# The pace of a projection stream in a chunked-scan block: one period for all steps, or one by the width of the step

## The chip, the cores and the metric

The kernel runs on one core of a Trainium2 chip. The metric is the device time of one execution in microseconds (us). Engines are named as in the profile: PE is TensorE (PEld its weight loads), DVE is VectorE, ACT is ScalarE, POOL is GpSimd, SP is SyncE, which issues the DMAs.

## What is computed

One layer of a diffusion block over 2048 latent tokens with a prefix of 256 context tokens, width 1024. One input projection feeds three groups of heads, whose outputs are joined, projected and followed by an MLP:

```python
zl = modulate(rms_norm(xl, p["norm1_g"]), ml[0], ml[1]) @ p["w_in"]
zl_gla, zl_rwkv, zl_ret = split_cols(zl, (GLA_COLS, RWKV_COLS, RET_COLS))
yl_gla, _ = gla_mixer(zl_gla, p, st_gla, True)          # gated linear attention, 4 heads
yl_rwkv, _ = rwkv7_mixer(zl_rwkv, p, st_rwkv, True, rows)  # RWKV-7, 6 heads
yl_ret, _ = retnet_mixer(zl_ret, p, st_ret, True, True)    # retention, 4 heads
xl = xl + ml[2] * (jnp.concatenate([yl_gla, yl_rwkv, yl_ret], axis=-1) @ p["w_out"])
hl = modulate(rms_norm(xl, p["norm2_g"]), ml[3], ml[4])
xl = xl + ml[5] * squared_relu_mlp(hl, p["mlp_w1"], p["mlp_w2"])
return rms_norm(xl, final_norm_g)
```

Each mixer scans the tokens forward and backward; the latent scans start from the final context states.

## The kernel before

The program has three parts: the modulation with that share of the input projection which RWKV needs first (to about 578 us of the span), the scans (to about 2075 us), and the output projection with the MLP (the rest). The change lies in the scans.

In the scans several generators write their instructions into one program, a step at a time: `prepare` (per direction, RWKV blocks: tiles `pg`, `p`, `M`, `X`, `XT`, `GB`, `BKT`), `chains` (the sequential RWKV chunks: `ptf`, `ptb`, `Ts`, `SUV`, `UV`, `py`), `inputs` (RWKV features of the second and third pair of heads: `px`, `pv`, `po`, `pl`), `finish` (`pm`, `pn`, `pgt`), `mix` (the GLA heads, `gpA`, `gpy`, `gpt`, `gz`, then two pairs of retention heads, `rpk`, `rpt`, `rpA`, `rpy`, with `fpt` at a head's end), and `ip_stream`, the projection stream of the title. All their matmuls have line L1068, that of a helper, so that the tiles' names tell them apart.

`ip_stream` (L445) computes the columns of the projection that GLA and retention need late: values, gates, and the retention's keys, values and queries. It goes through five groups of columns, `STREAM_T` (L442), and in each through the 18 tiles of 128 tokens (16 where context tokens aren't needed). Groups 0, 1, 2 and 4 are 384 columns wide (in 2 and 4 the two context tiles have 256), group 3 is 256 wide. For a tile it loads `rh` (512 KB, the saved normalized tokens as two fp16 parts; two buffers), makes 24 fp16 matmuls into `pz` (one buffer) with the weights `rwh` and `rwl`, scales `pz` to `rzs` on ACT and stores that to `zt` in DRAM. A `yield` after every sixth matmul makes four steps of a tile. The low half of a group's weights, `rwl`, is loaded into the buffer that the group before has just left (L454, three buffers).

An object of class `Order` (L1042) picks whose step is written next. It keeps a time `t` of its own, which grows with each matmul by a cost that goes by its columns. The other streams are picked by their position and by when their last step should be done. The projection stream has a `period`: it is taken when it is due, and ahead of that only where nothing else is ready and it is due within three periods:

```python
for s in paced:
    if s.due <= self.t or len(open_) == 1:
        return s
...
for s in paced:
    if s.due <= self.t + 3 * s.period:
        return s
...
if s.period:
    s.due = max(s.due, self.t - s.period) + s.period
```

`mix` waits for groups: the GLA heads for group 0, their last step (`follow`) for group 1, the first retention pair for the tiles of group 2 and at its end for group 3, the second pair for the tiles of group 4. What the generators write is then recorded by the framework, which may still move an instruction within an engine's order.

Of the kernel before, what the change touches and what calls it, by code (L numbers as in the profile page):

```python
# [366 lines left out]
def ip_tile(k, nm, wp, ps, tag="pn"):  # L367

    srcs, M, _ = CT[nm]
    wh = wp.tile([P, KD, P], F16, tag="wh", name="wh", bufs=3)  # L370
    wl = wp.tile([P, KD, P], F16, tag="wl", name="wl", bufs=3)
    return wh, wl, ip_weights(k, wp, ps.tile([P, 512], F32, tag=tag, name="pnrm")[:, 0:1], wh[:, :, 0:M], wl[:, :, 0:M], srcs, M)
# [59 lines left out]
def h_save(k, first):  # L432

    for ti in range(NT):
        with k.tc.issue_after(k.stores[first + ti]):
            for i, h in enumerate((k.hh, k.hl)):
                k.nc.sync.dma_start(k.hd[ti, :, i], h[:, :, ti * P : ti * P + P])
# [9 lines left out]
def ip_stream(k, wp, ps):  # L447


    nc = k.nc  # L450

    def weights(g, i):
        w = wp.tile([P, KD, 384], F16, tag="rw", name="rw" + "hl"[i], bufs=3)
        nc.sync.dma_start(w[:, :, 0 : P * len(STREAM_T[g])], k.wsd[g][i])  # L454
        return w

    wh = weights(0, 0)
    for g, cols in enumerate(STREAM_T):
        W, kind = P * len(cols), cols[0][2]
        wl = weights(g, 1)  # L460
        if g == 0:
            yield 8
        for ti in range(2 if kind == "g" else 0, NT):
            n = 256 if ti < 2 and kind == "r" else W
            if ti == NT - 1:
                nxt = weights(g + 1, 0) if g + 1 < len(STREAM_T) else None
            h = wp.tile([P, 2, KD, P], F16, tag="rh", name="rh", bufs=2)
            nc.sync.dma_start(h, k.hd[ti])
            pz = ps.tile([P, 512], F32, tag="fl", name="pz")
            i = 0  # L470
            for a, b in ((0, wh), (0, wl), (1, wh)):
                for kk in range(KD):
                    nc.tensor.matmul(pz[:, 0:n], h[:, a, kk, :], b[:, kk, 0:n], start=(i == 0), stop=(i == 23))
                    i += 1
                    if i in (6, 12, 18):
                        yield 0
            s = 1 if ti < 2 else 0
            zs = wp.tile([P, 384], F32, tag="rzs", name="rzs", bufs=2)
            for u in range(n // P):
                nc.scalar.activation(zs[:, P * u : P * u + P], pz[:, P * u : P * u + P], AF.Copy, scale=k.siv[:, g, u, s : s + 1])  # L480
            z = zs[:, 0:n]
            if kind == "g":
                th = wp.tile([P, 384], F32, tag="rth", name="rth")[:, 0:n]
                nc.scalar.activation(th, z, AF.Tanh, scale=0.5)
                nc.gpsimd.tensor_scalar(th, th, 0.5, 0.5, ALU.mult, ALU.add)
                nc.gpsimd.tensor_mul(z, z, th)
            nc.sync.dma_start(k.zt[ti * P : (ti + 1) * P, cols[0][1] : cols[0][1] + n], z)
            k.tile = ti + 1
            yield 0
        k.streamed, k.tile = k.streamed + 1, 0  # L490
        wh = nxt
# [57 lines left out]
def rw_weights(k, cp):  # L549

    nc = k.nc
    k.w3 = cp.tile([96, 3, 384], F32R, name="w3")
    with k.tc.tile_pool(name="rws", bufs=1) as tp:
        t = tp.tile([96, 3, 384], F32, name="w3f")
        for i, w in enumerate((k.I["rwkv_w2"][0, 0], k.I["rwkv_w2"][0, 1], k.I["rwkv_a2"][0])):
            for p in range(3):
                nc.sync.dma_start(t[32 * p : 32 * p + 32, i, :], w)
        stacked_rhs(nc, k.w3, t)
# [472 lines left out]
class Stream:  # L1031
# [5 lines left out]

    def pos(self):
        return self.first + (self.last - self.first) * self.done / self.count


class Order:  # L1042
# [1107 lines left out]
def tile_hybrid_block(ctx: ExitStack, tc: tile.TileContext, I, cst_ap, off, out):  # L2150
    nc = tc.nc
    k = K()
# [22 lines left out]
    with ExitStack() as rs:  # L2175
        rp = rs.enter_context(tc.tile_pool(name="rconst", bufs=1))
        cs = rp.tile([P, n_rw], F32, name="cst")
        nc.sync.dma_start(cs, cst_ap[:, 0:n_rw])
        k.cst = lambda n: cs[:, off[n][0] : off[n][0] + off[n][1]]
        k.gmax = rp.tile([R2, 4, NT, 2], F32, name="gmax")  # L2180
        feat = ExitStack()
        with ExitStack() as es:
            wp = es.enter_context(tc.tile_pool(name="ipw", bufs=2, side="right"))
            k.stores, k.turned, names = [], [], ["L", "G", "k0", "v0", "r0"]
            with tc.tile_pool(name="ipx", bufs=2) as xp, tc.tile_pool(name="mops", bufs=4, space=PSUM) as mps:
                ready = []
                first, rest = modulation1(k, xp, mps, lambda: ready.append(ip_tile(k, names[0], wp, mps, "pb")))
                hp, lp = (es.enter_context(tc.tile_pool(name="hT" + i, bufs=1, side="right")) for i in "hl")
                ips = es.enter_context(tc.tile_pool(name="ipps", bufs=2, space=PSUM, side="right"))
                k.hh = hp.tile([P, KD, T], F16, name="hT_hi")  # L2190
                k.hl = lp.tile([P, KD, T], F16, name="hT_lo")
                for i, bi in enumerate(TOK_ORDER):
                    h_block(k, bi, xp, None if i else first)
                    if i == 0:
                        with tc.issue_after(k.h_last):
                            rest()
                            ready.append(ip_tile(k, names[1], wp, mps, "pb"))
                    if i == 1:
                        ready.append(ip_tile(k, names[2], wp, mps, "pb"))
            k.ipn = es.enter_context(tc.tile_pool(name="ipn", bufs=1, space=PSUM, side="right"))  # L2200
            ip_channels(k, names, wp, ips, ready)
            setup(k)
            rw_setup(k, rp)
            h_save(k, 5)
            p0 = feat.enter_context(tc.tile_pool(name="rf0", bufs=1))
            p1 = feat.enter_context(tc.tile_pool(name="rf1", bufs=1))
            rw_weights(k, p0)
            rw_seg(k, p0)
            k.fb = 2
            with tc.tile_pool(name="rfb", bufs=2) as pool, tc.tile_pool(name="rfps", bufs=3, space=PSUM) as fps, tc.tile_pool(name="rbaps", bufs=1, space=PSUM) as bps:  # L2210
                rw_shared(k, pool)
                for _ in rw_inputs(k, 0, pool, pool, fps):
                    pass
                for _ in rw_base(k, 0, k.LTc, p1, bps):
                    pass
                ip_channels(k, ["k1", "v1", "r1"], wp, ips)
                modulation2(k, cp, 20)
                for _ in rw_inputs(k, 1, p1, pool, fps, 0, B1):
                    pass
                ip_channels(k, ["k2", "v2", "r2"] + GLA_COLS, wp, ips)  # L2220

        lps = rs.enter_context(tc.tile_pool(name="lps", bufs=2, space=PSUM))

        def inputs():
            pool = feat.enter_context(tc.tile_pool(name="rf", bufs=2))
            k.fb = 1
            yield from rw_inputs(k, 1, p1, pool, lps, B1)
            yield from rw_base(k, 1, k.LTc, p1, lps)
            k.inputs = 1
            yield from rw_inputs(k, 2, p1, pool, lps)  # L2230
            yield from rw_base(k, 2, k.LTc, p1, lps)
            feat.close()
            k.inputs = 2

        def mix():
            yield lambda: k.inputs == 2
            yield from mixers(k, lps)

        with ExitStack() as es:
            bp = es.enter_context(tc.tile_pool(name="rb", bufs=2, side="right"))  # L2240
            ps = es.enter_context(tc.tile_pool(name="rbps", bufs=3, space=PSUM, side="right"))
            fp = es.enter_context(tc.tile_pool(name="ipr", bufs=1, side="right"))
            fps = es.enter_context(tc.tile_pool(name="iprps", bufs=1, space=PSUM, side="right"))
            k.order, k.inputs, k.streamed, k.tile, k.fin = Order(nc), 0, 0, 0, None
            rw_scan(k, bp, ps)
            k.order.add(inputs(), 0, 108, 200, 12)
            k.mix = k.order.add(mix(), 108, 316, 270, 12)
            k.order.add(ip_stream(k, fp, fps), 0, 312, 345, period=3.1)
            k.order.run()
        gla_flag(k, cp)  # L2250
    gflag = nc.values_load(k.gflag, min_val=0, max_val=1)
# [30 lines left out]
```

## Time and profile before

| | |
|---|---|
| time, median of 3 runs | 3627.11 us (3613.73 to 3627.25) |
| the profiled execution: its time / span | 3641.55 us / 3639.4 us |
| mean granted clock of TensorE | 0.913 |
| busy: PE, DVE, ACT, POOL | 92%, 66%, 39%, 19% |
| PE records (an fp32 matmul is two) | 23600 |

The profile is of one execution. PE is busy nearly all the time, but a busy PE is not PE at its full clock: where the granted clock is 0.50, the chip runs TensorE at 1.2 of its 2.4 GHz, and the same matmuls take about twice as long. So the scans are read by stretches, each with its length, PE's busy time and the granted clock.

### The profile page before, as it was taken

To read this page: it belongs to the slowest core of one execution; us is meant where nothing else is said; L and a number is where in the kernel's file an instruction comes from. 1 tells how busy PE (TensorE), PEld (TensorE's weight loads), DVE (VectorE), ACT (ScalarE), POOL (GpSimd) and SP (SyncE) were. 2 spreads that over 40 slices of the span, in tenths; PEclk is the share of its full clock that TensorE was granted. 3 is DMA by queue.
4 is the path that set the end of the run, shared out by engine and by line. 5 is a ranking of instruction groups with operands and counts; after the bars stand their busy time and mean duration, and the time that the engine had idled before them with its cause. 6 is when DMAs were issued, how large, how long until landed. Compare 5 with 4: busy or idle time off the path is not lost. (4 is left out here: it accounts for less than half of the span.)

```text
span 3639.4 us, 62904 instructions
## 1 busy us (share of the span) xinstructions
PE 3362.6 (92%) x23600; PEld 2257.2 (62%) x23600; DVE 2388.7 (66%) x5128; ACT 1427.0 (39%) x3161; POOL 685.8 (19%) x863
## 2 busy tenths in 40 slices
PE   6798999998998999999999689799999999999997
PEld 2444445666675667777676577556666666666665
DVE  7458784767865667666656378777777764454446
ACT  3355553444434464443434234444433441122113
POOL 3224442324522223323222100000000010000001
PEclk7898999999987988778998599899999999999998
DMA  7988877536645245242523168744433473232232
GB/s 229 201 242 247 251 213 209 162 99 194 167 140 135 78 126 147 68 110 92 151 77 102 57 195 229 241 176 142 172 141 136 155 228 116 90 118 93 90 102 89
DMA packets 534345, 547.09 MB, mean 150 GB/s; under 512 B 276603, under 2 KB 407494, under 8 KB 533262
## 3 DMA queue, kind: packets, MB, share of 16 engines
q1 hardware_dynamic: 534032, 542.99, 50.1%
q8 instruction: 188, 3.08, 0.3%
q14 instruction: 125, 1.02, 0.1%
HBM read 331.18 MB, written 187.55 MB: 143 GB/s over the span
## 5 line engine op out<-in xcount | busy, mean ns | idle before, releaser
L1938 PE MATMUL pu<-H,wo 128*128 128x512 f16 x2688 | 608.7, 380 | 1.2 <-DVE s L1946 1.2
L2125 DVE TENSOR_TENSOR acc<-acc,pz 128x512 f32<-128x512 f32 x512 | 348.6, 686 | 348.3 <-PE pz L2123 346.5
L1938 PEld LDWEIGHTS <-wo 128*128 128x128 f16 x2688 | 252.0, 98 | 320.4 <-issue 41.1
L2123 PE MATMUL pz<-w2h,uh 128*128 128x512 f32 x1024 | 425.2, 419 | 11.7 <-ACT uh L1965 10.5
L2123 PE MATMUL pz<-w2l,uh 128*128 128x512 f32 x1024 | 403.4, 394 | 0.0
L2123 PE MATMUL pz<-w2h,ul 128*128 128x512 f32 x1024 | 397.3, 391 | 0.4 <-DVE ul L1967 0.4
L1068 PE MATMUL pz<-rwh,rh 128*128 128x384 f16 (+1 forms) x1376 | 294.5, 345 | 12.6 <-DMA rh<-hd 6.2
L1068 PEld LDWEIGHTS <-rh 128*128 128x128 f16 x2064 | 200.9, 106 | 137.8 <-issue 37.0
L2139 POOL TENSOR_TENSOR acc<-acc,fg 128x1024 f32<-128x1024 f32 x10 | 23.6, 2377 | 1373.9 <-ACT acc L2138 1373.9
L2123 PEld LDWEIGHTS pz<-w2h,uh 128*128 128x128 f32 x1024 | 194.0, 189 | 65.6 <-ACT uh L1965 11.5
L2123 PEld LDWEIGHTS pz<-w2h,ul 128*128 128x128 f32 x1024 | 192.9, 188 | 42.8 <-DVE ul L1967 1.1
L2123 PEld LDWEIGHTS pz<-w2l,uh 128*128 128x128 f32 x1024 | 194.2, 190 | 40.1
L425 PEld LDWEIGHTS <-wh 128*128 128x128 f16 (+2 forms) x1072 | 111.5, 108 | 148.5 <-issue 40.8
L1962 ACT ACTIVATE u<-u 128x512 f32<-128x512 f32 x64 | 36.8, 623 | 402.9 <-DVE s L1956 402.9
L425 PE MATMUL pz<-hT_hi,wh 128*128 128x512 f16 (+5 forms) x536 | 125.1, 374 | 41.4 <-ACT zs L428 23.5
L1068 PE MATMUL pz<-rwl,rh 128*128 128x384 f16 (+1 forms) x688 | 146.1, 343 | 0.0
L1068 PE MATMUL pg<-Z,BK 64*128 64x128 f32 (+1 forms) x864 | 131.3, 329 | 3.8 <-issue 1.1
L1950 ACT ACTIVATE s<-pu,iv 128x512 f32<-128x512 f32 x96 | 65.2, 684 | 166.3 <-PE pu L1938 163.9
L2043 PE MATMUL pz<-woh,yh 128*128 128x512 f32 x256 | 100.9, 409 | 30.7 <-DMA x<-in_w_out_dram 22.0
L425 PE MATMUL pz<-hT_hi,wl 128*128 128x512 f16 (+5 forms) x536 | 123.4, 368 | 0.0
L425 PE MATMUL pz<-hT_lo,wh 128*128 128x512 f16 (+5 forms) x536 | 121.4, 365 | 0.0
L1068 PEld LDWEIGHTS pg<-Z,BK 64*128 64x128 f32 x864 | 111.4, 226 | 15.0 <-issue 6.9
(522 smaller groups left out, 6920.4 us busy)
## 6 DMA issues: line engine op xcount, KB each, us to landing
rh<-hd SPq DMA_DIRECT2D x86, 512.0 KB
st<-in_mlp_w_dram SPq DMA_DIRECT2D x64, 512.0 KB
w1d<-wo SPq DMA_DIRECT2D x112, 256.0 KB
wo<-w1d SPq DMA_DIRECT2D x112, 256.0 KB
x<-in_x_dram SPq DMA_DIRECT2D x32, 512.0 KB
mw<-in_mod_w_dram SPq DMA_DIRECT2D x32, 512.0 KB
w2d<-w2h SPq DMA_DIRECT2D x32, 512.0 KB
w2d<-w2l SPq DMA_DIRECT2D x32, 512.0 KB
```

Source lines behind the costliest of these rows:

```text
L425: nc.tensor.matmul(pz[:M, o : o + step], a[:, kk, 0:M], b[:, kk, t0 + o : t0 + o + step], start=(i == 0), stop=(i == 23))
L1068: return op(out, lhs, rhs, **kw)
L1938: nc.tensor.matmul(bank, W[o][:, a, kk], H[o][:, 4 * b + kk], start=(i == 0), stop=(i == 11))
L1950: nc.scalar.activation(s, product(o), AF.Copy, scale=iv)
L1962: nc.scalar.activation(r, r, AF.Relu)
L2043: nc.tensor.matmul(pz, a[:, kk], w[:, kk, 512 * hf : 512 * hf + 512], start=(kk + i == 0), stop=(kk == KD - 1 and i == 2))
L2123: nc.tensor.matmul(pz, U[q][tb][u][:, ts], W2[q][w][:, cs], start=(i == 0), stop=(i == 5))
L2125: nc.vector.tensor_add(a[:, cs], a[:, cs], pz)
L2139: nc.gpsimd.tensor_mul(a, a, fg)
```

## The change

The stream's period is no longer 3.1 of the planner's units for every step, but 3.3 for a step of 384 columns and 2.2 for one of 256. `ip_stream` sets it at the first step of each tile, when the due time of that step has been set already.

```diff
@@ ip_stream
         for ti in range(2 if kind == "g" else 0, NT):
             n = 256 if ti < 2 and kind == "r" else W
+            k.stream.period = PACE * n / 384
@@ before class Order
+PACE = 3.3
@@ tile_hybrid_block
-            k.order.add(ip_stream(k, fp, fps), 0, 312, 345, period=3.1)
+            k.stream = k.order.add(ip_stream(k, fp, fps), 0, 312, 345, period=PACE)
```

No instruction is added or removed; they stand in another order. Lines after L462 are one higher in the changed kernel, those after `PACE` four (the helper's L1068 is L1072). PE's matmul instructions in the scans, counted in its order from one group's last stream matmul to the next one's last:

| part of PE's order | all matmuls, before | now | of these the stream's | share of the stream, before | now |
|---|---|---|---|---|---|
| group 0 (384 wide) | 1715 | 1580 | 432 | 0.252 | 0.273 |
| group 1 (384) | 1530 | 1709 | 384 | 0.251 | 0.225 |
| group 2 (384) | 1606 | 1378 | 432 | 0.269 | 0.313 |
| group 3 (256) | 1862 | 1625 | 384 | 0.206 | 0.236 |
| group 4 (384) | 1694 | 1899 | 432 | 0.255 | 0.227 |
| behind the stream | 238 | 454 | 0 | 0 | 0 |

PE, at the change from group 0 to group 1, before; between the two stream matmuls stand 16 others:

```order
L1068 MATMUL pz<-rwh,rh 128x384
L1068 MATMUL p_8664<-XT,M_8611 64x32 x8
L1068 MATMUL py<-Z,SUVf 64x64
L1068 MATMUL ptf<-Tsf,XT 64x64 x2
L1068 MATMUL ptb<-Tsb,XT 64x64 x2
L1068 MATMUL py<-Z,SUVf 64x64
L1068 MATMUL py<-Z,SUVb 64x64 x2
L1068 LDWEIGHTS rh
```

Now, from the same stream matmul on:

```order
L1072 MATMUL pz<-rwh,rh 128x384
L1072 MATMUL pg<-Z,BK 128x128 x4
L1072 MATMUL py<-Z,SUVf 64x64
L1072 MATMUL ptf<-Tsf,XT 64x64 x2
L1072 MATMUL py<-Z,SUVf 64x64
L1072 MATMUL pv<-ident,v 128x128 x3
L1072 MATMUL ptb<-SUVb,Z 64x64 x2
L1072 MATMUL py<-Z,SUVb 64x64 x2
L1072 MATMUL ptb<-Tsb,XT 64x64 x2
L1072 MATMUL p_8449<-X,GB 64x64 x8
```

These rows are the beginning of 145 matmuls of RWKV and its features that now stand between the two groups.

PE, in group 3, the beginning of its longest run without a stream matmul, before (286 matmuls to the next one):

```order
L1068 MATMUL pz<-rwh,rh 128x256
L1068 MATMUL p_17138<-M_17066,XT 64x32 x8
L1068 MATMUL p_17149<-XT,M_17066 64x64 x8
L1068 MATMUL p_17159<-M_17101,XT 64x32 x8
L1068 MATMUL ptf<-UVf,BKT 64x64 x2
L1068 MATMUL ptb<-UVb,BKT 64x64 x2
L1068 MATMUL gpy<-gV,gAs_17350 128x96
L1068 MATMUL p_17170<-XT,M_17101 64x64 x8
```

Now the longest run of group 3 has 148:

```order
L1072 MATMUL pz<-rwh,rh 128x256
L1072 MATMUL p_16968<-X,GB 64x64 x8
L1072 MATMUL ptf<-UVf,BKT 64x64 x2
L1072 MATMUL ptb<-UVb,BKT 64x64 x2
L1072 MATMUL gpA<-gqm,gkm 128x128 x4
L1072 MATMUL py<-Z,SUVf 64x64 x2
L1072 MATMUL py<-GB,UVf 64x64 x2
L1072 MATMUL gpA<-gqm,gkm 128x128
```

The run of 286 is gone; group 3 holds the same 384 stream matmuls among 237 fewer others.

PE, behind the stream's last matmul, before:

```order
L1068 MATMUL pz<-rwh,rh 128x384
L1068 MATMUL ptf<-Tsf,XT 64x64 x2
L1068 MATMUL ptb<-Tsb,XT 64x64 x2
L1068 MATMUL fpt<-ident,rY 128x128 x4
L1068 MATMUL py<-GB,UVf 64x64
L1068 MATMUL py<-GB,UVb 64x64
L1068 MATMUL ptf<-UVf,BKT 64x64 x2
```

Now:

```order
L1072 MATMUL pz<-rwh,rh 128x384
L1072 MATMUL py<-Z,SUVf 64x64 x2
L1072 MATMUL py<-GB,UVf 64x64 x2
L1072 MATMUL rpk<-rV,rkd 64x64
L1072 MATMUL py<-Z,SUVb 64x64 x2
L1072 MATMUL py<-GB,UVb 64x64 x2
L1072 MATMUL p_21949<-M_21870,XT 64x32 x8
```

The stream now ends while RWKV blocks are still being prepared (`p`); 216 matmuls more stand behind it.

## Rows read from the trace of the kernel before

**Rows 1.** The page: the span, and busy time of each engine.

```profile
span 3639.4 us, 62904 instructions
...
PE 3362.6 (92%) x23600; PEld 2257.2 (62%) x23600; DVE 2388.7 (66%) x5128; ACT 1427.0 (39%) x3161; POOL 685.8 (19%) x863
```

**Rows 2.** The tile `rwh`: its matmuls (ns min/median/max, first and last start).

```profile
L1068 PE MATMUL pz<-rwh,rh x1376: 269/326/543, 577.7 to 1978.2; 128*128 128x384 f16 x151, 128*128 128x256 f16 x46
```

**Rows 3.** The tile `rwl`: the loads of groups 1 to 4.

```profile
L454 SPq DMA_DIRECT2D rwl<-ws1l x1: 320/320/320, 843.6 to 843.6; - x1
L454 SPq DMA_DIRECT2D rwl<-ws2l x1: 319/319/319, 1075.8 to 1075.8; - x1
L454 SPq DMA_DIRECT2D rwl<-ws3l x1: 562/562/562, 1362.6 to 1362.6; - x1
L454 SPq DMA_DIRECT2D rwl<-ws4l x1: 320/320/320, 1719.3 to 1719.3; - x1
```

**Rows 4.** Windows, one per group and the tail: length, busy us (records), clock, DMA.

```profile
core 0: us, PE busy (x) PEld busy (x) DVE busy (x) ACT busy (x) POOL busy (x), PEclk, DMA share, GB/s
577.70:843.60 265.90, 249.24 (x2752) 173.51 (x2751) 166.48 (x402) 104.87 (x335) 77.67 (x124) 0.92 0.49 139
843.60:1075.80 232.20, 217.72 (x2411) 152.21 (x2409) 182.71 (x475) 100.22 (x312) 107.24 (x137) 0.90 0.60 172
1075.80:1362.60 286.80, 261.33 (x2799) 186.78 (x2797) 185.69 (x462) 145.21 (x373) 75.08 (x111) 0.88 0.43 115
1362.60:1719.30 356.70, 331.14 (x3219) 264.62 (x3218) 242.34 (x647) 149.60 (x376) 114.11 (x159) 0.77 0.38 103
1719.30:1978.20 258.90, 250.26 (x2852) 185.86 (x2851) 150.28 (x494) 98.87 (x305) 61.08 (x68) 0.93 0.38 113
1978.20:2075.00 96.80, 77.90 (x390) 65.36 (x389) 44.89 (x139) 28.95 (x63) 19.96 (x20) 0.52 0.14 42
```

**Rows 5.** Waits of PE from 577 to 2075 us: total, times, longest.

```profile
PE fpt L1068 <- POOL rY L1477: 10.6, 4, 7.7
PE pk L1068 <- ACT sqf L781: 9.0, 3, 4.2
PE pu L1068 <- DMA gz<-gzsl: 7.2, 2, 4.2
PE pz L1068 <- DMA rh<-hd: 6.2, 4, 1.9
...
PE pz L1068 <- ACT rzs L480: 5.5, 6, 2.9
```

**Rows 6.** Windows over the longest runs without a stream matmul (columns as above).

```profile
1517.50:1577.60 60.10, 60.10 (x564) 51.25 (x564) 25.05 (x71) 11.26 (x37) 13.93 (x16) 0.57 0.22 57
1392.80:1414.10 21.30, 21.30 (x307) 18.15 (x307) 11.40 (x33) 6.31 (x18) 8.24 (x9) 1.00 0.48 93
1922.30:1941.50 19.20, 17.31 (x246) 15.12 (x247) 7.93 (x25) 4.88 (x18) 2.79 (x3) 0.80 0.30 88
```

**Rows 7.** Windows at the end of the scans (columns as above).

```profile
2000.00:2025.00 25.00, 20.25 (x89) 17.31 (x89) 16.41 (x53) 8.21 (x17) 5.82 (x7) 0.50 0.11 32
2025.00:2050.00 25.00, 25.00 (x118) 22.84 (x119) 4.14 (x8) 7.46 (x14) 2.80 (x3) 0.50 0.00 1
2050.00:2075.00 25.00, 13.23 (x60) 11.25 (x58) 9.01 (x20) 2.21 (x4) 6.89 (x5) 0.50 0.13 44
```

## The prediction, made before the changed kernel was run

> **What bounds the kernel now.** I read the page first: PE is busy for 3362.6 of 3639.4 us [rows 1], so this is a kernel whose time is PE's, and the question is where PE waits and where it runs slowly. The chain of waits ends in the last normalization and says nothing of the scans, so I cut the scans into stretches. The stream's first matmul starts at 577.7 us and its last at 1978.2 [rows 2]; the low half of each group's weights is loaded when the group before has given its buffer back, at 843.6, 1075.8, 1362.6 and 1719.3 us [rows 3]. These marks make six windows [rows 4]: five groups, and a tail in which no stream is left. PE is busy 91 to 97% of each group, and its single waits are small: the largest kind adds up to 10.6 us over the whole of the scans [rows 5]. What differs is the granted clock: 0.92, 0.90, 0.88 and 0.93 in the wide groups 0, 1, 2 and 4, but 0.77 in the narrow group 3, and 0.52 in the tail [rows 4]. At half clock (1.2 GHz) nearly every matmul takes twice as long, so the clock is what the order can gain or lose.
>
> Divided by the matmuls that stand in PE's order (the table of the change), the windows of [rows 4] cost, for each matmul: group 0 265.9/1715 = 0.155 us, group 1 232.2/1530 = 0.152, group 2 286.8/1606 = 0.179, group 3 356.7/1862 = 0.192, group 4 258.9/1694 = 0.153, the tail 96.8/238 = 0.407.
>
> **The change, part by part.** It adds no instruction. A step of 384 columns comes 3.3/3.1 = 6% later in the planner's time, one of 256 comes 29% sooner. What this does is seen in the order: group 3 sheds 237 other matmuls, the wide groups together take 21 more (6545 before, 6566 now), and the tail 216 more. Within the wide groups it is uneven: groups 1 and 4 get thinner (the stream's share falls from 0.251 and 0.255 to 0.225 and 0.227), groups 0 and 2 denser (0.252 and 0.269 to 0.273 and 0.313). So there are four terms.
>
> *(a) The wide groups.* No row shows a wide group with a share of 0.226; the nearest are groups 1 and 4 at 0.253 with a mean clock of 0.915, and group 3 at 0.206 with 0.77 [rows 4]. On the line between these, 0.027 less share costs 0.027 x 0.145/0.047 = 0.083 of clock. Groups 1 and 4 now hold 3608 matmuls at 0.152 us, 549 us; at a clock of 0.832 in place of 0.915 that is +55. The denser groups 0 and 2 hold 2958 at 552.7/3321 = 0.166 us, 492 us; at best their clock goes from 0.90 to the 0.93 of group 4, -16. Together +39 at most. At the other end stands 0: among the wide groups the rows show no slope at all (group 2 has the largest share and the lowest clock). I take **+24**, above the middle, since 0.226 lies between the two rows and not beyond them.
>
> *(b) The narrow group.* Its longest run without the stream, 286 matmuls, took 60.1 us at a clock of 0.57, with PE busy all the time; a run of 159 took 21.3 us at full clock, 0.134 each, as which the 286 would be 38.3 us [rows 6]. That run is broken up; the longest is now 148. If the loss goes with it, -22. If the same matmuls are as slow elsewhere, 0, for they don't vanish. I take the middle, **-11**.
>
> *(c) The tail.* 216 matmuls move from stretches at 1400.5/8407 = 0.167 us each (36 us) to a place with no stream between them. Their price there: 0.134 as in the run at full clock, 29 us; 0.210 (60.1/286) as in the run at 0.57 [rows 6], 45 us; or 0.407 as in the tail now, 88 us. Net -7, +9 or +52. I take **+9**: the clock of the tail, 0.52 and 0.50 to its end [rows 4, 7], is that of the middle row, but the tail's 0.407 is the price of the retention's last, serial pieces, and what is added are RWKV's blocks and chunks.
>
> *(d) The stream's loads.* Each tile's `rh` is one DMA of SP's queue, and SP issues it in the stream's place. In the narrow group these now follow each other faster. PE waited for `rh` four times, 6.2 us in all, at most 1.9 [rows 5], out of 86 loads. All 16 narrow tiles waiting 1.9 us would be +30, none 0; with four in 86 I take **+1**. The wait of `pz` for its scaling on ACT, 5.5 us in all [rows 5], is the same in kind and stays in this.
>
> The sum is 24 - 11 + 9 + 1 = +23 us. Against the profiled execution's own 3641.55 us that is 3664.6; that execution is 14 us above the median of the runs shown, 3627.11, so the time I forecast is **3650 us**.
>
> **A rule to weigh.** PE was busy for 60.10 of 60.10 us in the long run of group 3, and the clock was 0.57 [rows 6]; in the last 25 us of the tail it was busy for 13.23 and the clock 0.50 [rows 7]. So here the clock falls with and without idle time. The Trainium skill ("TensorE: Matmul & The Clock Gate", section "Why this matters for your kernels") says that a drop in mid-kernel is avoided by leaving TensorE no long idle gap between bursts of matmuls. By that rule a thinner stream costs nothing as long as PE has other work, so that (a) and (b) would be 0 and the sum +10; the trace disagrees in the first of these rows and agrees in the second.
>
> **The rivals.**
>
> *Faster: the narrow group recovers.* If the clock of group 3 follows its share on the same line, 0.206 to 0.236 gives 0.093 more, 0.863; its 1625 matmuls at 0.192 us are 311 us and become 278, -34. If groups 1 and 4 keep their clock (a = 0) and the tail's price is the lowest (-7), that is -41: 3586 us. For it speaks the line itself, which I used for the wide groups. Against it: group 2 had the largest share and still 0.88, and group 3 without its long run was at (0.77 x 356.7 - 0.57 x 60.1)/296.6 = 0.81 [rows 4, 6], so that the GLA heads' own matmuls seem to cost clock whatever the stream does. It decides from the point where groups 1 and 4 stay at 0.88 or above. Chance 0.2.
>
> *No difference.* The clock goes by idle gaps, or what the wide groups lose group 3 gains: a + b = 0, and c and d leave +10: 3637 us. That the change doesn't do what it says belongs here: the period might hardly bind, since a ready stream is also taken up to three periods ahead. But 237 matmuls have left group 3, so it binds. Chance 0.2.
>
> *Slower still: the tail.* The 216 matmuls behind the stream run at the tail's own 0.407 us, because chunks wait for each other with nothing to fill PE: c = +52, the sum 24 - 11 + 52 + 1 = +66: 3693 us. For it speaks the tail's PE, busy 77.9 of 96.8 us [rows 4]; against it, that these matmuls still stand beside the second retention pair. Chance 0.1.
>
> **How the numbers follow.** The forecast has 0.5. With (a) between +12 and +33, (b) between -20 and 0 and (c) between 0 and +25, not all at one end, its own range is 3632 to 3672. A measurement of this kernel tells about 0.5%, 18 us, from no change. The forecast lies above that for 0.36 and within it for 0.14; the faster rival lies below it for 0.19 and within it for 0.01, no difference within it for 0.12 and above for 0.08, the tail's rival above. So faster 0.19, the same 0.27, slower 0.54. The range for 8 in 10, 3600 to 3690 us, leaves out the outer part of the faster rival (0.13) and half of the tail's (0.05).
>
> **What would show it.** Right: groups 1 and 4 at a clock of 0.81 to 0.88, a tail of more than 120 us (96.8 + 216 x 0.134 = 126 at full clock), no run of 60 us at 0.57, and group 3 at 1625 matmuls in about 300 us. Wrong: a clock of 0.90 in groups 1 and 4, or of 0.86 in group 3, which is the faster rival; a tail over 160 us, which is the slower one; or new waits of PE for `rh` or `rwl` of more than 10 us, which none of these has.

## The result, and the profile after

The changed kernel takes 3649.11 us (median of 12 runs, 3630.26 to 3668.31), the kernel before 3625.89 us in the 12 runs beside it (3611.72 to 3648.83): a ratio of 1.0058, 95% interval 1.0035 to 1.0081. That is 23 us slower, the forecast's sum almost to the microsecond. The first two profiles say something else: both executions have a span of 3639.4 us. Single executions of one order differ by 10 to 50 us here, so each kernel was profiled three times; the first profile of the change is shown, and means are of three. All ratios and means in this document leave out five executions of the kernel before that were over 1.5% above the fastest of their round.

The page, after (span; busy time of each engine), for [rows 1]:

```profile
span 3639.4 us, 62912 instructions
...
PE 3346.1 (92%) x23600; PEld 2245.9 (62%) x23600; DVE 2393.0 (66%) x5128; ACT 1423.5 (39%) x3161; POOL 682.6 (19%) x863
```

Windows, after: groups 0 to 4 and the tail, cut as [rows 4] at the loads of `rwl` and at the stream's first and last matmul.

```profile
core 0: us, PE busy (x) PEld busy (x) DVE busy (x) ACT busy (x) POOL busy (x), PEclk, DMA share, GB/s
578.60:828.50 249.90, 234.62 (x2569) 162.30 (x2569) 158.94 (x371) 99.77 (x318) 71.29 (x119) 0.95 0.51 142
828.50:1089.90 261.40, 243.31 (x2858) 175.57 (x2859) 206.69 (x555) 112.03 (x350) 114.86 (x149) 0.90 0.56 163
1089.90:1346.00 256.10, 227.83 (x2213) 162.05 (x2212) 149.89 (x350) 125.48 (x321) 66.28 (x97) 0.86 0.45 118
1346.00:1677.00 331.00, 299.94 (x2800) 235.61 (x2800) 224.58 (x596) 143.25 (x343) 99.25 (x147) 0.75 0.40 104
1677.00:1955.10 278.10, 268.18 (x3180) 201.99 (x3178) 166.00 (x505) 97.67 (x319) 73.17 (x83) 0.95 0.37 109
1955.10:2075.70 120.60, 97.34 (x806) 79.16 (x804) 70.97 (x245) 45.76 (x112) 27.35 (x26) 0.68 0.19 60
```

Against [rows 4]: group 4 holds more work and runs at 0.95, group 3 holds 237 matmuls less and still stands at 0.75, the tail is 24 us longer but at 0.68 in place of 0.52.

Waits of PE, after, from 577 to 2075 us (total, times, longest):

```profile
PE fpt L1072 <- POOL rY L1481: 10.3, 4, 7.7
PE ptf L1072 <- DVE SUVf L977: 7.7, 8, 1.7
PE py L1072 <- DVE UVf L966: 7.0, 3, 3.6
...
PE pz L1072 <- DMA rh<-hd: 3.3, 4, 1.5
```

No single kind of wait has grown to matter, and the stream's loads cost 3.3 us where they cost 6.2 [rows 5].

Windows, after: the 58 us at half clock in group 3, the longest run of that group without a stream matmul (columns as above), and the last 100 us.

```profile
1374.10:1432.10 58.00, 56.55 (x348) 45.82 (x344) 25.53 (x70) 7.88 (x27) 12.90 (x14) 0.50 0.18 43
...
1559.30:1582.10 22.80, 22.80 (x289) 19.80 (x287) 12.09 (x43) 5.04 (x16) 5.25 (x6) 0.72 0.28 60
...
1975.00:2000.00 25.00, 19.17 (x211) 14.20 (x210) 22.69 (x95) 17.28 (x44) 3.10 (x5) 0.90 0.22 70
2000.00:2025.00 25.00, 23.41 (x133) 18.69 (x132) 11.86 (x41) 5.77 (x16) 3.38 (x4) 0.50 0.10 32
2025.00:2050.00 25.00, 25.00 (x111) 22.26 (x110) 8.05 (x33) 6.36 (x13) 3.41 (x4) 0.50 0.05 17
2050.00:2075.00 25.00, 13.77 (x82) 10.92 (x81) 9.59 (x21) 4.88 (x8) 7.91 (x6) 0.70 0.13 43
```

The run of 286 matmuls [rows 6] is gone, and what took its place is another stretch of 58.0 us at half clock, with PE busy for 56.55 of it: it lies 137 us earlier, in a piece of the GLA heads that the stream does break up. Behind the stream the clock is 0.90 first (1975 to 2000 us), then it falls to 0.50 as it did before [rows 7].

**Three ways to lose time.** From the windows the scans' time can be split: PE's idle time (length less busy), what the low clock takes (length times one minus the granted clock), and the rest, which is the same work at full clock.

| sums over the six windows, us (three profiles) | before | after |
|---|---|---|
| PE idle | 109.7, 107.8, 105.1 | 125.9, 121.1, 123.5 |
| taken by the low clock | 225.5, 219.5, 234.2 | 209.7, 222.2, 224.0 |
| rest | 1162.1, 1156.7, 1157.9 | 1161.5, 1154.8, 1159.0 |
| length of the scans | 1497.3, 1484.1, 1497.2 | 1497.1, 1498.1, 1506.5 |

The rest is the same to 0.1% (1158.9 and 1158.4 in the mean). The change adds 16 us of idle time in the mean, 13 to 18 in the pairs, and in these three takes 8 off the clock's share: 8 us in all, where the medians differ by 23.

The other 15 us lie in which executions were profiled. The granted clock is on record for every execution of the change and of the experiments. The three profiled ones of before had 0.911 to 0.915, while its 58 executions beside the experiments average 0.917; the three of the change average 0.915, as do the 12 of which the median is taken. Split in the same way over the whole kernel, an execution of before loses 300.0 us to the low clock and takes 3324.1 for all else, idle time included; one of the change 311.0 and 3336.4 (standard errors 2 and 4 us for the clock, 1 and 2 for all else). So of the 23 us, 11 are low clock and 12 are other time, most likely the idle time that the profiles show.

The split takes half clock to double the time, and that is a little too much. The same PE instructions in the same order, without a pause, in the first profile of before at full clock and in its second at half (columns as above):

```profile
1869.20:1877.90 8.70, 8.70 (x111) 7.76 (x111) 3.29 (x11) 3.77 (x10) 2.45 (x3) 1.00 0.28 86
1851.50:1867.20 15.70, 15.70 (x111) 13.63 (x110) 3.29 (x11) 3.93 (x11) 3.47 (x4) 0.50 0.14 47
```

That is a factor of 1.80; over 36 such pairs of pieces, from the three profiles of either kernel, it is 1.76 (1.56 to 1.84). With 1.76 the clock's share shrinks by 14%, and the 23 us are about 10 of clock and 14 of other time.

### The profile page after: what moved, and what is told of

Same layout as the page of the kernel before. It is cut to its first block, busy times and chain, and to the rows that moved or that the text cites. A ratio compares the mean times of both kernels' runs of the same rounds, so it can differ in the third digit from the quotient of the medians.

```text
span 3639.4 us, 62912 instructions
## 1 busy us (share of the span) xinstructions
PE 3346.1 (92%) x23600; PEld 2245.9 (62%) x23600; DVE 2393.0 (66%) x5128; ACT 1423.5 (39%) x3161; POOL 682.6 (19%) x863
## 5 line engine op out<-in xcount | busy, mean ns | idle before, releaser
L1072 PE MATMUL pz<-rwh,rh 128*128 128x384 f16 (+1 forms) x1376 | 287.5, 339 | 6.5 <-DMA rh<-hd 3.3
L1072 PEld LDWEIGHTS <-rh 128*128 128x128 f16 x2064 | 198.7, 105 | 127.3 <-issue 25.7
L1072 PE MATMUL pz<-rwl,rh 128*128 128x384 f16 (+1 forms) x688 | 141.3, 337 | 0.0
L1072 PE MATMUL pg<-Z,BK 64*128 64x128 f32 (+1 forms) x864 | 122.4, 311 | 6.5 <-DMA Z<-AR 2.1
L425 PE MATMUL pz<-hT_lo,wh 128*128 128x512 f16 (+5 forms) x536 | 121.1, 364 | 0.0
L1072 PEld LDWEIGHTS pg<-Z,BK 64*128 64x128 f32 x864 | 101.7, 208 | 19.9 <-issue 8.3
```

Source lines behind the costliest of these rows:

```text
L425: nc.tensor.matmul(pz[:M, o : o + step], a[:, kk, 0:M], b[:, kk, t0 + o : t0 + o + step], start=(i == 0), stop=(i == 23))
L1072: return op(out, lhs, rhs, **kw)
```

## The experiments

All of them set the period by group, in place of the changed line. The number of matmuls in groups 0 to 4 and the tail is counted in PE's order, as in the table of the change. Ratios are to the kernel before in the same round (there were three, each on a chip of its own), with 95% intervals. Windows are of one profiled execution each. After the first two, three theories stood: **early** (the pace of the first wide groups costs in itself), **place** (a matmul's price goes by the part it stands in, dear beside the GLA heads) and the forecast's **share** (a thinner stream lowers the clock of its group).

**1. early_wide: the wide pace alone, in groups 0 to 2** (1580, 1709, 1378, 1932, 1796, 250).

```diff
+            k.stream.period = 3.3 * n / 384 if g < 3 else 3.1
```

> Groups 0 to 2 as in the changed kernel (period 3.3, context tiles 2.2, the same order of PE up to there), groups 3 and 4 at 3.1 as before: 250 matmuls behind the stream, as good as before (238). Forecast (the thin wide groups cost, and most of it in group 1, whose share of 0.225 it has): the wide term without that of group 4, about +10 to +20 us, 3636 to 3646. Faster rival (wide groups keep their clock, the gain is group 3's): 3626, no difference. Tail rival (all of the loss is behind the stream): 3626, no difference.

3687.6 us, ratio 1.0156 (1.0111 to 1.0200): slower than the change itself, and far above every expectation. Its windows for group 3, and two stretches in it:

```profile
1349.20:1763.90 414.70, 377.65 (x3328) 297.63 (x3329) 261.22 (x697) 156.04 (x382) 117.49 (x167) 0.68 0.33 89
...
1376.70:1438.10 61.40, 60.05 (x380) 48.49 (x379) 27.60 (x79) 9.07 (x29) 15.33 (x17) 0.50 0.21 53
1697.50:1758.90 61.40, 61.14 (x399) 49.33 (x400) 25.98 (x73) 11.20 (x40) 13.67 (x15) 0.50 0.15 46
```

The loss sits behind the edit, in group 3: 414.7 us for 1932 matmuls, with two stretches of 61.4 us at half clock where before had one of 58.0.

**2. narrow_only: the narrow pace alone, in group 3** (1715, 1530, 1606, 1405, 1607, 782).

```diff
+            k.stream.period = 2.2 if g == 3 else 3.1
```

> Groups 0 to 2 as before to the instruction; group 3 at 2.2 with 1405 matmuls in place of 1862, group 4 at 3.1, and 782 matmuls behind the stream, 544 more. Forecast: group 3 -11, the tail 544/216 x 9 = +23: +12 us, 3638. Faster rival: group 3 at a share of 0.273 goes to a clock of 0.93, 269 us become 223, and the tail costs nothing more: -46 to -64, 3562 to 3580. Tail rival: 544 x (0.407 - 0.167) = +131 less 11: 3746.

3634.06 us, 1.0011 (0.9985 to 1.0036): no difference. Its windows of group 3 and the tail:

```profile
1341.80:1606.90 265.10, 243.59 (x2364) 191.56 (x2364) 178.85 (x490) 115.24 (x278) 89.29 (x128) 0.80 0.46 122
...
1880.20:2071.10 190.90, 163.13 (x1406) 133.22 (x1404) 104.13 (x352) 66.94 (x167) 44.83 (x46) 0.68 0.18 54
```

The clock of group 3 rises to 0.80 and some 90 us leave it [rows 4]; a tail of 782 matmuls takes them back.

**3. third_wide: group 2 alone at 3.3, its context tiles too** (1715, 1530, 1610, 1619, 1969, 202): the change's narrow group in size, without its early groups and its tail.

```diff
+            k.stream.period = 3.3 if g == 2 else 3.1
```

> Only group 2 goes at 3.3, all else at 3.1. Groups 0 to 2 then hold the matmuls of before (1715, 1530, 1610); group 3 holds 1619 in place of 1862, as few as in the change, group 4 1969 in place of 1694, the tail 202 in place of 238. So this is the change's narrow group without its early groups and without its tail. Theory 'place' (a matmul costs 0.19 to 0.2 us in group 3, beside the GLA heads, and 0.15 in group 4, whatever the stream's share): group 3 about 316 us, group 4 about 295, tail about 90; 701 us against 713 before, so about 3615 us. Rival 'share' (the forecast's line: group 4's share 0.219 takes 0.11 from its clock, group 3's 0.237 gives 0.09): group 3 about 283, group 4 about 342 at a clock near 0.81, tail 90; 3627 us with a clock of 0.86 in group 3. Rival 'early' (only the pace of groups 0 and 1 costs): 3627 us.

3610.08 us, 0.9958 (0.9927 to 0.9989). Groups 3 and 4:

```profile
1352.20:1650.20 298.00, 268.31 (x2746) 210.05 (x2745) 222.25 (x588) 139.67 (x338) 101.86 (x145) 0.84 0.44 115
1650.20:1953.20 303.00, 288.13 (x3365) 214.34 (x3364) 180.09 (x573) 112.38 (x349) 72.29 (x80) 0.94 0.35 106
```

Group 4 has a share of 0.219 and a clock of 0.94: the line from share to clock is refuted. Group 3 holds as many matmuls as in the change (1619, 1625) at 0.84 in place of 0.75. So the number of matmuls in a group doesn't set its clock. That it is their order is likely, but not shown by this.

**4. two_wide: groups 0 and 1 at 3.3** (1580, 1709, 1422, 1485, 2164, 285).

```diff
+            k.stream.period = 3.3 if g < 2 else 3.1
```

> Groups 0 and 1 at 3.3, all others at 3.1. Groups 0 and 1 hold what they hold in the change and in early_wide (1580, 1709), group 2 1422, group 3 only 1485, group 4 2164, the tail 285. Theory 'early' (what early_wide lost was lost by the pace of groups 0 and 1, whatever follows): about 3685 us, as early_wide. Theory 'place' (it was lost by the 1932 matmuls of its group 3): groups 0 and 1 515 us, group 2 266, group 3 290, group 4 2164 x 0.15 = 325, tail 100; 1496 us as in the change, so 3640 to 3650 us. Rival 'share': group 4, with a share of 0.200, falls to a clock near 0.75 and takes 406 us; about 3725 us.

3630.81 us, 1.0015 (0.9978 to 1.0053). Theory *early* falls, and *share* with it: group 4, at 0.200 of stream, is at 0.89.

```profile
1353.80:1617.70 263.90, 240.04 (x2494) 188.15 (x2492) 192.65 (x510) 122.00 (x294) 95.60 (x136) 0.85 0.46 120
1617.70:1958.20 340.50, 329.46 (x3697) 250.67 (x3698) 209.42 (x632) 130.93 (x393) 82.96 (x93) 0.89 0.33 101
```

It differs from experiment 1 by the pace of group 2 alone. That is worth 57 us between the medians, 51 by the ratios: there, pacing group 2 by width loses, while in experiment 3 a longer period in all tiles of group 2 gains 15 by the ratio.

**5. after_g4: the change without its tail** (groups 0 to 3 of the change; 2123 in group 4, 230 behind the stream).

```diff
-            k.stream.period = PACE * n / 384
+            k.stream.period = 4.0 if g == 4 else 3.3 * n / 384
```

> The change with group 4 at 4.0 in place of 3.3. Groups 0 to 3 are those of the change to the instruction; 224 matmuls move from behind the stream into group 4 (2123 there, 230 in the tail, as before). Theory 'place': group 4 gains 224 x 0.15 = 34 us, the tail loses 33 (120.6 to about 88); 3649 us, as the change. Theory 'tail' (the matmuls behind the stream are the dear ones, at 0.266 us each): 34 us more in group 4, 60 fewer behind it; about 3623 us. Rival 'share' (0.203 in group 4, clock near 0.76): group 4 about 393 us, tail 88; about 3731 us.

3681.2 us, 1.0162 (1.0115 to 1.0209): 32 us slower than the change. Group 4 and the tail:

```profile
1675.90:2022.90 347.00, 329.52 (x3590) 246.64 (x3590) 200.73 (x618) 118.34 (x373) 80.77 (x89) 0.87 0.32 97
2022.90:2109.40 86.50, 60.60 (x378) 49.26 (x376) 43.41 (x129) 26.59 (x57) 19.93 (x20) 0.72 0.14 44
```

Against the change's means (278.3 and 119.3 us) the 224 matmuls cost 69 us more in group 4, 0.31 each, and give back 33 behind it, 0.15 each. No theory had that: the tail is the cheaper place for them. *Place* falls as a price list too, since group 4 was to take them at 0.15.

**6. late_wide: the change's late part alone** (1715, 1530, 1606, 1405, 1759, 630).

```diff
+            k.stream.period = (3.1, 3.1, 3.1, 2.2, 3.3)[g]
```

> Groups 0 to 2 at 3.1, group 3 at 2.2, group 4 at 3.3: the change without its early pace, or narrow_only with 152 matmuls moved from the tail (782 to 630) into group 4 (1607 to 1759). Theory 'early': the change's loss is gone, and 152 matmuls cost 0.15 in group 4 in place of 0.244 in the tail; 3634 - 14 = 3620 us. Theory 'place': the same 3620 us, with group 3 at 265 us, group 4 near 296 and the tail near 154. Rival 'share' (0.246 in place of 0.269 in group 4 takes 0.07 from its clock): group 4 about 325 us, tail 154; about 3649 us, the change's own time.

3613.36 us, 0.9972 (0.9940 to 1.0004). Groups 3, 4 and the tail:

```profile
1339.70:1587.90 248.20, 230.44 (x2364) 181.40 (x2364) 181.94 (x491) 114.77 (x278) 88.44 (x128) 0.85 0.50 131
1587.90:1876.90 289.00, 270.15 (x2970) 200.25 (x2971) 163.06 (x472) 104.97 (x319) 69.09 (x83) 0.87 0.32 95
1876.90:2032.40 155.50, 131.93 (x1127) 105.37 (x1124) 94.55 (x324) 57.87 (x146) 36.11 (x36) 0.72 0.22 65
```

So the paces of groups 3 and 4 don't cost the 23 us; what the change does ahead of them does. Against experiment 2 the 152 matmuls that left the tail give 35 us there and cost 16 in group 4, about the 20 us between the medians. But these are single profiles, and group 3, the same to the instruction in both, took 265.1 us there and 248.2 here, so the match may be chance.

**7. first_two_even: the change with groups 0 and 1 put back** (1715, 1530, 1618, 1531, 1856, 395). A theory for it was *runs*: no pace has a price, the half-clock stretches of the GLA part have one.

```diff
-            k.stream.period = PACE * n / 384
+            k.stream.period = 3.1 if g < 2 else 3.3 * n / 384
```

> The change with groups 0 and 1 alone put back to 3.1; groups 2, 3 and 4 keep the change's periods (3.3, 2.2, 3.3, and 2.2 at the context tiles). Groups 0 and 1 are then before's to the instruction, group 2 holds 1618 matmuls, group 3 1531, group 4 1856, the tail 395. Theory 'runs' (no period has a price of its own; what costs is the low clock behind stretches of the GLA part in which no stream matmul stands, and those come and go with the order): groups 0 and 1 496 us, group 2 about 275, group 3 1531 x 0.18 = 276, group 4 1856 x 0.158 = 293, tail about 110; 1450 us of scans against 1484 to 1497 before, about 3605 us. Rival 'price' (3.3 in the wide groups costs as such, 2.2 in the narrow one gains): the change without the 13 us that its groups 0 and 1 were longer than by before's prices; about 3636 us, no different from before.

3646.42 us, 1.0061 (1.0035 to 1.0086): as slow as the change. Groups 2 and 3:

```profile
1070.40:1356.10 285.70, 258.01 (x2849) 186.24 (x2847) 192.87 (x477) 145.61 (x377) 75.59 (x113) 0.92 0.44 117
1356.10:1668.40 312.30, 283.19 (x2626) 219.99 (x2627) 193.96 (x532) 136.75 (x330) 96.66 (x145) 0.74 0.41 106
```

Both expectations miss. *Runs* was too hopeful: 1531 matmuls at 0.18 us, and they took 0.204, as the change's did, at a clock of 0.74. The trace has one long stretch at half clock in that group, with PE busy throughout:

```profile
1516.80:1568.00 51.20, 51.20 (x350) 40.91 (x346) 20.43 (x59) 8.64 (x29) 10.73 (x13) 0.50 0.27 60
```

The pace of groups 0 and 1 is cleared a second time. And against experiment 6 only group 2 is paced otherwise, with the two context tiles of group 4: 32 us by the ratios, the second pair in which pacing group 2 by width loses.

**8. narrow_g4: experiment 6 with group 4 at 3.7** (1715, 1530, 1606, 1405, 1835, 554).

```diff
+            k.stream.period = (3.1, 3.1, 3.1, 2.2, 3.7)[g]
```

> late_wide with group 4 at 3.7 in place of 3.3: 76 matmuls more move from the tail (630 to 554) into group 4 (1759 to 1835); groups 0 to 3 are those of late_wide and narrow_only. Theory 'runs': a matmul costs about 0.15 us in either place as long as no new low-clock stretch opens; 3613 us, as late_wide. Rival 'group 4' (matmuls pushed into group 4 cost what the 224 of after_g4 cost there, 0.31 us each, and 0.15 in the tail): 3613 + 76 x 0.16 = 3625 us.

3594.36 us (3586.17 to 3637.17), 0.9919 (0.9889 to 0.9948): the lowest median of the ten orders, 32 us below before and 55 below the change (its interval overlaps those of experiments 3 and 6). Its profiled execution is the slowest of its seven, 3637.17 us, and so doesn't show the gain. Groups 3 and 4, and a stretch of group 4 with 11.2 us on either side:

```profile
1354.00:1604.30 250.30, 232.17 (x2364) 182.59 (x2363) 179.54 (x487) 114.62 (x278) 87.91 (x128) 0.84 0.49 130
1604.30:1935.80 331.50, 317.16 (x3120) 237.52 (x3120) 173.44 (x518) 111.06 (x337) 72.19 (x85) 0.80 0.30 89
...
1641.10:1652.30 11.20, 11.20 (x97) 8.12 (x98) 10.38 (x37) 4.12 (x15) 2.87 (x3) 1.00 0.52 148
1652.30:1727.40 75.10, 75.10 (x493) 56.76 (x492) 24.69 (x58) 11.09 (x41) 13.92 (x14) 0.50 0.16 47
1727.40:1738.60 11.20, 11.20 (x97) 8.40 (x96) 5.60 (x12) 2.32 (x10) 0.00 (x0) 1.00 0.37 113
```

Group 3 is that of experiment 6; the excess is in group 4, at a clock of 0.80 in this execution, with 75.1 us at half clock in one piece. PE has no pause ahead of that piece nor in it, and 43 matmuls of the stream stand in it. Where the median's gain over experiment 6 comes from is not shown.

**9. Both kernels unchanged, profiled a second and a third time.**

> The kernel before once more, for a second profile of it. Its first profiled execution (3641.6 us) was 16 us above its median, that of the changed kernel (3641.3) 8 us below its own, so that the two profiles are equally long and say little on the 23 us between the medians. All theories: a time of 3612 to 3649 us as in the twelve runs; stretches of groups 0 to 4 and the tail within some 10 us of 266, 232, 287, 357, 259 and 97. If a stretch differs by more than that, it is the one in which executions of one kernel differ, and a difference between the two kernels there needs more than one profile each.

> The changed kernel once more, for a second profile. All theories: 3630 to 3668 us. Forecast: group 1 and group 4 together longer than before by some 50 us and more, group 3 shorter by about 40, the tail longer by about 45 less the work that moved. Faster rival: group 3 at a clock of 0.86. Tail rival: a tail over 160 us.

> The kernel before once more, for a third profile of the same order. If the split of its scans is a property of the order, idle time of PE in them is 108 to 110 us as in the two profiles so far, and what the low clock takes (length times one minus the granted clock, summed over the six windows) is 219 to 226. If single executions scatter in the clock, the second number moves by more than 10 us and the first does not.

> The changed kernel once more, for a third profile of the same order. If the change adds idle time to PE, it is again 121 to 126 us in the scans; if the rest of the 23 us is the clock, what the low clock takes is about 8 us more than before's mean; so far it is 210 and 222, against 226 and 220 before.

Before 3630.48 and 3642.56 us, after 3644.20 and 3653.77. The table above has the numbers. The idle time holds to 5 us in each kernel (105.1 lies just below what was expected of before, 123.5 is within); the clock's share scatters by 15, and in the third pair it is lower in the changed kernel, not 8 us higher.

**All orders side by side.** Clocks of groups are of one profiled execution (before and after: of three). The low clock's share and all else are means over all executions, in us of the whole kernel, split as above (standard errors 2 to 9 and 1 to 3).

| order (periods of groups 0 and 1; 2; 3; 4) | ratio | low clock | all else | clock of group 2 | of group 3 | of group 4 |
|---|---|---|---|---|---|---|
| 3.3; by width; 2.2; 4.0 (experiment 5) | 1.0162 | 326.3 | 3353.6 | 0.83 | 0.79 | 0.87 |
| 3.3; by width; 3.1; 3.1 (1) | 1.0156 | 344.8 | 3341.9 | 0.87 | 0.68 | 0.88 |
| 3.1; by width; 2.2; by width (7) | 1.0061 | 304.9 | 3338.7 | 0.92 | 0.74 | 0.92 |
| 3.3; by width; 2.2; by width (the change) | 1.0058 | 311.0 | 3336.4 | 0.83 to 0.86 | 0.75 | 0.93 to 0.96 |
| 3.3; 3.1; 3.1; 3.1 (4) | 1.0015 | 287.7 | 3337.8 | 0.86 | 0.85 | 0.89 |
| 3.1; 3.1; 2.2; 3.1 (2) | 1.0011 | 285.6 | 3345.1 | 0.92 | 0.80 | 0.88 |
| 3.1 throughout (before) | 1 | 300.0 | 3324.1 | 0.88 to 0.91 | 0.76 to 0.78 | 0.88 to 0.93 |
| 3.1; 3.1; 2.2; 3.3 (6) | 0.9972 | 276.4 | 3335.9 | 0.95 | 0.85 | 0.87 |
| 3.1; 3.3; 3.1; 3.1 (3) | 0.9958 | 262.9 | 3346.2 | 0.94 | 0.84 | 0.94 |
| 3.1; 3.1; 2.2; 3.7 (8) | 0.9919 | 267.5 | 3332.8 | 0.89 | 0.84 | 0.80 |

From before to the change one can go through the table a step at a time:

| step | time | low clock | all else |
|---|---|---|---|
| group 3 to 2.2 (before to 2) | +6.5 | -14.4 | +21.0 |
| group 4 to 3.3 (2 to 6) | -18.4 | -9.2 | -9.2 |
| group 2 by width, with group 4's two context tiles (6 to 7) | +31.3 | +28.5 | +2.8 |
| groups 0 and 1 to 3.3 (7 to the change) | +3.8 | +6.1 | -2.3 |
| all | +23.2 | +11.0 | +12.3 |

So on this way the one step that costs time clear of the scatter is the pace of group 2, and its price is low clock. The narrow pace of group 3 takes 14 us off the clock and adds 21 elsewhere. From experiment 4 to 1, the other such pair, low clock takes 57 us more and all else 4. Another sequence of steps could divide the sum otherwise.

The four orders in which group 2 goes by width (3.3, and 2.2 at its two context tiles) are the four slowest, with no exception; in them group 3 stays at 0.68 to 0.79, and in the other five changed orders it is at 0.80 to 0.85. The kernel before, at 0.76 to 0.78, stands with the first four. What parts them in the traces is one long stretch: group 3 has 51 to 61 us at half clock in one piece in each of these four (experiment 1 has two) and in all three profiles of before and of the change, and in the other five no piece above 34.1. This split was seen with the results at hand, not forecast. Whether the context tiles' 2.2 does it, or 3.3 only in company with other edits, is open: no run has group 2 at 3.3 throughout together with the change's other paces.

## Why the prediction came out right, and where it was wrong

The total is right: 3650 forecast, 3649.11 measured, and slower was the side with the most chance. Its terms are not. Priced as the forecast did, each part's new count at its price per matmul of before (all of them means of three profiles):

| part | before, us | after, us | after's count at before's price | difference |
|---|---|---|---|---|
| group 0 | 264.7 | 250.5 | 243.9 | +6.6 |
| group 1 | 229.7 | 265.3 | 256.6 | +8.7 |
| group 2 | 281.1 | 256.1 | 241.2 | +14.9 |
| group 3 | 355.5 | 331.0 | 310.3 | +20.7 |
| group 4 | 265.1 | 278.3 | 297.2 | -18.9 |
| tail | 96.8 | 119.3 | - | +22.5 in all |

- **(a) the wide groups**, forecast +24, come to +11, inside the bounds of 0 to +39, but by the opposite of the reason given. The step that failed is the line from share to clock: the thinner groups 1 and 4 were to lose 55 us and gained 10 together (group 4 at 0.93 to 0.96), the denser 0 and 2 were to gain 16 and lost 21.5. Experiments 4 and 7 clear the pace of groups 0 and 1; experiments 3 and 4 show thin groups 4 at 0.94 and 0.89.
- **(b) the narrow group**, forecast -11 with bounds of -22 and 0, is +21. The step "that run is broken up; if the loss goes with it" failed: the run went, the low clock didn't. The change has its 58.0 us at half clock elsewhere in the group. That clock is to be gained there was right, as the faster rival said: group 3 is at 0.80 to 0.85 in experiments 2 to 4, 6 and 8, but not behind the change's group 2.
- **(c) the tail**, forecast +9 with bounds of -7 and +52, is -24. Both prices were too high for it. Its 216 matmuls cost 22.5 us, 0.104 each, below the lowest row (0.134); and what left came from the dear groups 2 and 3: the moves among the five groups, at each one's own price of before, are worth -46.9 us, not the -36 of a mean price. Experiment 5 says the same: sent back into group 4, such matmuls cost twice as much as here.
- **(d) the stream's loads**, forecast +1: 3.3 us of waiting in place of 6.2, as small as forecast, with the other sign.

The sum of the three profiles is then 11 + 21 - 24 = +8 us, and the scans did grow by 7.7 (1492.9 to 1500.6). The median says +23. So the match of the total is luck in good part: terms that are off by 13 to 33 us cancel in these profiles, and about half of the 23 us isn't clock at all. The profiles have it as 16 us of PE idle, 4 to 6 each in groups 1 and 3 and the tail; of PE's waits the forecast priced those of the stream alone, in (d). The prediction's "takes twice as long" at half clock is too much as well: 1.76 times, as shown above.

The signs named beforehand read as follows. For the forecast: a tail over 120 us (119.3, borderline), no run of 60 us without the stream at 0.57 (right as written, but 58.0 us at half clock stand elsewhere). Against it: group 4 at 0.95, and group 3 at 331 us for the "about 300". The faster rival's point of decision, groups 1 and 4 at 0.88 or more, was met in the mean of each and the kernel was still slower, because group 3 didn't follow the line.

**The rule that was weighed**, by which (a) and (b) were 0 and the sum +10, misses too: the interval of the ratio is 13 to 29 us. Idle time alone doesn't tell where the clock falls. Matmuls of the GLA heads ran at full clock in group 2 of before, and at half clock in the same part of the change (windows, columns as above: first before, with its half-clock stretch of group 3 under it; then after, and the same place in the change's third profile).

```profile
1247.40:1281.00 33.60, 33.30 (x441) 27.16 (x440) 17.74 (x47) 9.37 (x35) 11.38 (x13) 1.00 0.36 85
...
1510.80:1568.80 58.00, 57.55 (x420) 47.95 (x420) 26.42 (x74) 9.11 (x30) 13.29 (x15) 0.50 0.22 57
```

```profile
1240.00:1251.20 11.20, 9.51 (x141) 8.39 (x139) 9.00 (x23) 2.28 (x5) 3.60 (x3) 1.00 0.01 1
1251.20:1281.80 30.60, 28.61 (x174) 24.07 (x174) 9.41 (x22) 4.62 (x17) 10.02 (x12) 0.50 0.24 43
...
1236.00:1247.20 11.20, 10.88 (x129) 8.56 (x127) 10.46 (x28) 2.88 (x7) 2.18 (x3) 1.00 0.07 23
1247.20:1295.00 47.80, 44.98 (x282) 37.23 (x282) 17.95 (x41) 9.38 (x29) 14.13 (x15) 0.50 0.36 72
```

PE was 99% busy in the first and 93% in the half-clock stretch of the change's first profile. Before has three runs of 8.5 to 9.6 us without the stream there; in the change the clock falls inside one of 22.3 us. PE was idle for 1.7 of the 11.2 us ahead of the fall in the first profile, but for 0.3 in the third. The Trainium skill ("TensorE: Matmul & The Clock Gate", section "Why this matters for your kernels") puts a drop in mid-kernel down to long idle gaps between bursts of matmuls. Here there is some idle time on the slow side, so these rows alone don't exclude it. The stretch of group 4 in experiment 8 does, for that place: PE was busy for 11.20 of the 11.20 us ahead of the fall and for 75.10 of the 75.10 us behind it. In group 3 PE was busy for 57.55 of 58.00 us before and for 56.55 of 58.00 after, so it isn't idle time that keeps the clock low there; but a gap of 1.4 to 2.6 us stands within 4 us of the start of these stretches, and whether it starts them was not tested.

**What stays open**: why group 2 by width leaves group 3 at 0.75 (context tiles or the rest), what makes the half-clock stretches, and how much of the 12 us beside the clock is the idle time of the profiles.

## What to carry to other kernels

A pace in a list scheduler has no price of its own: by the ratios, the step from 3.1 to 3.3 in group 2 was worth -15 us alone and, with 2.2 at its context tiles, +32 and +51 beside other paces. Forecast such a change from the order it makes, place by place, and don't draw a line between two groups that differ in everything else; then try several settings one group at a time, since the best of ten lay 55 us below the change and 32 below the kernel before. Where one order's executions differ by as much as the effect, profile it more than once before reading a window, and compare the profiled execution's clock with that of the others.

## What the runs showed of the hardware

- One order, one chip, and 3586.17 to 3637.17 us: the executions of experiment 8 go with the mean granted clock, 0.931 in the fastest and 0.915 in the slowest. The rest of the scans' time, with idle and low clock taken off, stayed between 1151 and 1171 us in all fourteen profiles, while the scans took 1455 to 1564, so that most of the difference between profiles is clock and idle time.
- At half clock the same PE instructions took 1.76 times as long (36 pairs of pieces, 1.56 to 1.84), not twice.
- The clock can fall, and stay low for 75.1 us, with PE busy all the time (experiment 8). The longest half-clock pieces of group 3 come back from execution to execution: 58.0, 61.4 and 58.0 us in before, 58.0 three times in the change and once in experiment 5, whose order is the same up to there. Matmuls of the same kind ran at full clock elsewhere.
- Matmuls put behind the stream cost 0.104 us each in the change, and 0.13 to 0.17 in experiments 2, 6, 7 and 8. In its first profile the change's first long piece at half clock comes 40 us into the tail (a short one of 17 us comes at 12 in the other two); before's comes 4 us into it.
